# Strassen block products in the up projection of the last layer's MLP of a two-layer diffusion trunk

## The chip, the cores and the metric

The kernel runs on one core of a Trainium2 chip. The metric is the device time in microseconds (us), the median of several runs. A core has five engines with a queue of instructions each, worked through in order: TensorE (PE, with its weight loads shown apart as PEld), VectorE (DVE), ScalarE (ACT), GpSimd (POOL) and SyncE (SP), which here only issues transfers. They wait for each other through semaphores. Sixteen DMA engines carry the transfers.

## The reference

Two layers work on 640 tokens (128 of a prompt, 512 of a sample) of 1024 features. What matters here is step 4 of each layer, a gated MLP with a depthwise convolution over neighbouring tokens; `D_FF` is 2816, and `w_up` has 5632 columns.

```
h2 = _rmsnorm(x, p['norm2']) * (1 + sc2) + sh2
a, g = jnp.split(_dwconv3(h2 @ p['w_up'], p['conv_w'], p['conv_b']), 2, axis=-1)
x = x + g2 * ((jax.nn.silu(a) * g) @ p['w_down'])
```

The convolution is done for the prompt and the sample apart, so nothing crosses the border between token 127 and token 128.

## The kernel before

Activations lie transposed, features on the 128 partitions and tokens along the free dimension. The hidden features come in 22 tile pairs: pair f is a tile of 128 columns of `a` and the tile of `g` that goes with it. Every product is made in three passes (`mm3`): a float32 operand is split into a high part and the small rest, and low times high, high times low and high times high are added up in PSUM.

A weight tile goes through a fixed chain (`load_w`). SP issues one transfer into a staging buffer `st`, ACT copies it to `wh` (the high part), DVE subtracts to get `wl` (the rest), and the matmuls read `wh` and `wl`. There are 3 buffers of `st` and 5 each of `wh` and `wl`, used in turn for all weights of the phase, so at most eight tiles are ahead of PE. A staging buffer is free again when its `wl` is made; a pair of `wh` and `wl` when its last matmul has run.

`mlp_up` does a pair: two weight tiles of 128 by 1024, each with 48 matmuls of 320 columns (2 token halves, 8 blocks of 128 features, 3 passes). ACT takes the sum out of PSUM twice, as `u` and as `v` times the middle tap; DVE adds the outer taps in four instructions (the segments 0 to 127 and 128 to 639 apart); then follow SiLU, the product with the gate, and a split into `ah` and `al`. The down projection (`dn`, and `dl` for the last group) follows each group of 6, 6, 5 and 5 pairs, eight output tiles each, with weights through the same chain. The order on each engine is set by a scheduler that moves instructions ahead as buffers allow.

Beside this, `mod_steps` computes the modulation vectors on DVE from `stm` loads: two DVE instructions of 1024 columns for each of 8 tiles of a group of features. Group 5 (the gate `g2` of the MLP) of the last layer is computed in the last layer's own MLP.

Of the kernel before, what the change touches and what calls it, by code (L numbers as in the profile page):

```python
# [20 lines left out]
P = 128  # L21
# [6 lines left out]
F_T = 22  # L28
EPS = 1e-6
GROUPS = [(0, 6), (6, 12), (12, 17), (17, 22)]  # L30
WINDOWS = (2, 4, 8, 16)
FILL = [[], [('u', 3), ('u', 2), ('u', 1)], [('u', 0), ('g', 16)], [('g', 17), ('g', 18), ('p', 3), ('p', 2)], [('g', 19), ('p', 1), ('p', 0)], [('g', 20), ('g', 8)], [('g', 9), ('g', 10)]]
REST = [('g', 11)]
# [23 lines left out]
def trunk_kernel(ctx: ExitStack, tc: tile.TileContext, a: dict):  # L57
# [10 lines left out]
    wp = tp("wp", 5)  # L68
    dram = (ctx.enter_context(tc.tile_pool(name="dram", bufs=1, space=DRAM)))
    ps_t = tp("ps_t", 2, space=PSUM)  # L70
    ps_a = tp("ps_a", 1, space=PSUM)
    ps_b = tp("ps_b", 1, space=PSUM)

    ident = const.tile([P, P], F32, name="ident")
    make_identity(nc, ident)
# [32 lines left out]
    def load_unit(l, u, eng=vec):  # L108
        return [load_w(a["w_unit"][l, u, c], 768, eng) for c in range(4)]

    def mm3(out, sh, sl, mh, ml, start, stop):
        pe.matmul(out, sl, mh, start=start, stop=False)  # L112
        pe.matmul(out, sh, ml, start=False, stop=False)  # L113
        pe.matmul(out, sh, mh, start=False, stop=stop)  # L114

    def powr(out, x):
        n = x.shape[1]
# [698 lines left out]
    def out_phase(l, x, rp, m32, hp, ps_d):  # L816
# [28 lines left out]
            modulate(rp, x, bc, A2, B2, a0, b0, h2h[c], h2l[c])  # L845
        return h2h, h2l

    def mlp_up(l, f, h2h, h2l, mp, ps_d):
# [21 lines left out]
        va, vg = vs  # L870
        after[0] = vg[:, 0:1]
        act.activation(va, va, AF.Silu)
        vec.tensor_tensor(out=va, in0=va, in1=vg, op=ALU.mult)
        ah = mp.tile([P, T], F32R, tag="ah", name="ah", bufs=8)
        al = mp.tile([P, T], F32R, tag="al", name="al", bufs=8)
        split(va, ah, al)
        return ah, al
# [8 lines left out]
    xst = ExitStack()  # L886
    xp = tp("xp", 1, xst)
    rp = tp("rp", 2, xst)
    x = xp.tile([P, ND, T], F32, name="x")
    hst = ExitStack()  # L890
    hp = tp("h1p", 1, hst, side="right")
# [79 lines left out]
    sst.close()  # L971
    for l in range(L):
        dst.close()
        xst.close()
        attention_phase(l, hh, hl, w0)
        w0 = None
        xst = ExitStack()
        xp = tp("xp", 1, xst)
        rp = tp("rp", 2, xst)
        modp = tp("modp", 1, xst)  # L980
        x = xp.tile([P, ND, T], F32, name="x")
        dst = ExitStack()
        ps_d = open_dense(dst)
        with ExitStack() as ms:
            mp = tp("mg", 1, ms)
            cs = modp.tile([P, 2, 1024], F32, tag="cs", name="cs", bufs=1)
            msteps = mod_steps(l, range(2, 6), modp, cs)
            m32 = merge_phase(l, x, cs, hh, hl, mp, ps_d, msteps)
            hst.close()
            hst = ExitStack()  # L990
            hp = tp("h2p", 1, hst, side="right")
            h2h, h2l = out_phase(l, x, rp, m32, hp, ps_d)
        with ExitStack() as ms:
            mp = tp("mlp", 1, ms)
            ups = {}
            if l + 1 < L:
                msteps = chain(msteps, mod_steps(l + 1, range(2), modp, cs))

            def up_to(f):
                for i in range(len(ups), f):  # L1000
# [4 lines left out]
            for gi, (f0, f1) in enumerate(GROUPS):  # L1005
# [17 lines left out]
                if l + 1 < L:  # L1023
                    hst = ExitStack()
                    hp = tp("h1p", 1, hst, side="right")
                    hh = hp.tile([P, ND, T], F32R, name="hh")
                    hl = hp.tile([P, ND, T], F32R, name="hl")
                    A1 = scale_cols(l + 1, V_N1, 8, "A1")
                for c, (a0, b0) in enumerate(CH_A):
                    acc = Acc(rp, b0 - a0)  # L1030
                    for n0 in range(0, 8, 2):
                        ps = ps_d.tile("dl")
                        for j in range(2):
                            n = n0 + j
                            hi, lo = load_w(a["w_down"][l, n, :, f0 * P:f1 * P], nf * P)
                            for i in range(nf):
                                ks = slice(i * P, (i + 1) * P)
                                mm3(ps[:, j, :b0 - a0], hi[:, ks], lo[:, ks], fs[i][0][:, a0:b0],
                                    fs[i][1][:, a0:b0], i == 0, i == nf - 1)
                            down_add(l, x, n, ps[:, j], a0, b0)  # L1040
                            if l + 1 < L:
                                acc.add(x[:, n, a0:b0], n == 7)
                                dma(x_dram[:, n, a0:b0], x[:, n, a0:b0])
                            else:
                                dma(a["y"][:, n, a0:b0], x[:, n, a0:b0])
                    if l + 1 < L:
                        rms1_chunk(l + 1, c, rp, x, hh, hl, ps_d, acc, A1)
    dst.close()
    xst.close()


# [110 lines left out]
```

## Time and profile before

| what | value |
|---|---|
| device time, three runs | 2299.66 us median (2299.19 to 2304.29) |
| device time of the profiled execution | 2307.55 us |
| span of the profiled execution, first to last instruction | 2305.3 us |
| PE, PEld, DVE, ACT, POOL busy | 97%, 94%, 68%, 42%, 23% of the span |
| last layer's MLP | from 1827 us to the end |

The page of the profile gives busy time by engine, groups of instructions with their mean duration, waits with the engine that ended them, and the transfers with their time from issue to landing. PE records overlap, since matmuls are pipelined: the cost of one matmul in a dense stretch is the stretch divided by its number of matmuls, not the duration of one.

### The profile page before, as it was taken

Reading aid. Unit: us, or ns where it says so; the run is one execution under the profiler, and the core shown is the slowest. Engines: PE = TensorE matmul, PEld = TensorE weight load, DVE = VectorE, ACT = ScalarE, POOL = GpSimd, SP = SyncE. Lnnn points to the kernel's source line nnn. Section 1 sums busy time; section 2 is a strip of 40 time slices with the busy share of each in tenths; the row PEclk is TensorE's granted clock in tenths of the full one; section 3 lists DMA queues with packets and bytes.
Section 4 is the critical chain, followed back from the end, with each engine's and each line's share of the span. In section 5 each row is a group of like instructions: output and inputs, shape, how many; then the busy total and the mean of one; then the engine's idle time right before and its main releaser. Section 6 shows DMA issues by size and latency. Waiting matters only on the chain. (4 is left out here: it accounts for less than half of the span.)

```text
span 2305.3 us, 37922 instructions
## 1 busy us (share of the span) xinstructions
PE 2225.9 (97%) x14778; PEld 2163.6 (94%) x14778; DVE 1562.8 (68%) x2913; ACT 975.7 (42%) x1728; POOL 528.4 (23%) x651
## 2 busy tenths in 40 slices
PE   8898999999999999999979999999999999999999
PEld 4898989989999999999969989899999999999999
DVE  6877687559567756765587867864895676554555
ACT  4555555432244423333355645653323453242422
POOL 3753443024041000000047533320422200000000
PEclk8999999999999999999999999999999999999999
DMA  7211223367333333432242112224762332322123
GB/s 256 80 57 59 82 66 107 108 244 228 121 121 106 101 104 121 135 102 88 75 128 83 57 49 83 97 89 135 283 210 89 123 110 92 94 65 90 50 84 114
DMA packets 102775, 258.50 MB, mean 112 GB/s; under 512 B 19523, under 2 KB 32579, under 8 KB 102596
## 3 DMA queue, kind: packets, MB, share of 16 engines
q1 hardware_dynamic: 102596, 256.09, 34.1%
q8 instruction: 116, 1.90, 0.3%
q14 instruction: 63, 0.51, 0.1%
HBM read 233.10 MB, written 22.95 MB: 111 GB/s over the span
## 5 line engine op out<-in xcount | busy, mean ns | idle before, releaser
L95 ACT ACTIVATE wh<-st 128x1024 fp32r<-128x1024 f32 (+3 forms) x336 | 314.7, 943 | 297.0 <-PE dn L114 170.8
L113 PE MATMUL up<-h2l,wh 128*128 128x320 f32 x1408 | 435.6, 310 | 2.5 <-DVE h2l L209 2.4
L112 PE MATMUL up<-h2h,wl 128*128 128x320 f32 x1408 | 433.5, 310 | 2.4 <-ACT v L862 1.4
L114 PE MATMUL up<-h2h,wh 128*128 128x320 f32 x1408 | 435.0, 310 | 0.0
L96 DVE TENSOR_TENSOR wl<-st,wh 128x1024 fp32r<-128x1024 f32 (+3 forms) x336 | 375.4, 1120 | 71.7 <-ACT wh L95 71.1
L113 PEld LDWEIGHTS up<-h2l,wh 128*128 128x128 f32 x1408 | 265.2, 189 | 3.6 <-DVE h2l L209 3.6
L112 PEld LDWEIGHTS up<-h2h,wl 128*128 128x128 f32 x1408 | 264.5, 189 | 4.0 <-ACT h2h L208 2.1
L114 PEld LDWEIGHTS up<-h2h,wh 128*128 128x128 f32 x1408 | 265.3, 189 | 0.1
L143 DVE SCALAR_TENSOR_TENSOR junk<-stm,cs 128x1024 bf16<-128x1024 f32 x172 | 223.2, 1298 | 60.1 <-DMA stm<-in_w_mod 57.2
L865 DVE SCALAR_TENSOR_TENSOR v<-u,vecs,v 128x127 f32<-128x127 f32 (+1 forms) x176 | 89.1, 547 | 183.4 <-ACT v L862 183.4
L112 PE MATMUL mm<-wh,hl 128*128 128x384 f32 x480 | 169.5, 353 | 15.0 <-ACT raw L361 10.8
L113 PE MATMUL dn<-al,wh 128*128 128x320 f32 x544 | 168.1, 309 | 0.0
L114 PE MATMUL dn<-ah,wh 128*128 128x320 f32 x544 | 168.1, 309 | 0.0
L112 PE MATMUL dn<-ah,wl 128*128 128x320 f32 x544 | 168.1, 309 | 0.0
L113 PE MATMUL mm<-wl,hh 128*128 128x384 f32 x480 | 163.7, 341 | 2.6 <-DVE wl L96 2.6
L114 PE MATMUL mm<-wh,hh 128*128 128x384 f32 x480 | 163.4, 340 | 0.0
L114 PE MATMUL gp<-hh,wh 128*128 128x320 f32 x480 | 148.6, 310 | 0.0
L112 PE MATMUL gp<-hh,wl 128*128 128x320 f32 x480 | 148.4, 310 | 0.0
L113 PE MATMUL gp<-hl,wh 128*128 128x320 f32 x480 | 148.3, 309 | 0.0
L112 PE MATMUL mmu<-hh,wl 128*128 128x384 f32 (+1 forms) x416 | 134.0, 322 | 4.0 <-ACT up L677 2.0
L114 PE MATMUL mmu<-hh,wh 128*128 128x384 f32 (+1 forms) x416 | 131.0, 315 | 0.0
L113 PE MATMUL mmu<-hl,wh 128*128 128x384 f32 (+1 forms) x416 | 130.4, 314 | 0.0
(226 smaller groups left out, 5444.6 us busy)
## 6 DMA issues: line engine op xcount, KB each, us to landing
stm<-in_w_mod SPq DMA_DIRECT2D x88, 512.0 KB, 4.3
st<-in_w_up SPq DMA_DIRECT2D x88, 512.0 KB, 3.6
st<-in_w_gate SPq DMA_DIRECT2D x48, 512.0 KB, 4.4
st<-in_w_unit SPq DMA_DIRECT2D x48, 384.0 KB, 3.2
st<-in_w_out SPq DMA_DIRECT2D x32, 512.0 KB, 3.6
st<-in_w_down SPq DMA_DIRECT2D x48, 320.0 KB, 3.0
st<-in_w_br SPq DMA_DIRECT2D x24, 512.0 KB, 3.6
st<-in_w_down SPq DMA_DIRECT2D x32, 384.0 KB, 3.2
```

What stands on the lines that cost most here:

```text
L95: act.activation(hi, x, AF.Copy)
L96: eng.tensor_tensor(out=lo, in0=x, in1=hi.bitcast(F32), op=ALU.subtract)
L112: pe.matmul(out, sl, mh, start=start, stop=False)
L113: pe.matmul(out, sh, ml, start=False, stop=False)
L114: pe.matmul(out, sh, mh, start=False, stop=stop)
L143: vec.scalar_tensor_tensor(out=junk, in0=st, scalar=1.0, in1=cs[:, j], op0=ALU.mult, op1=ALU.mult, accum_out=col)
L865: vec.scalar_tensor_tensor(out=v[:, s + 1:e], in0=u[:, s:e - 1], scalar=cw[0], in1=v[:, s + 1:e], op0=ALU.mult, op1=ALU.add)
```

## The change

Only the last layer's MLP and its surroundings change. The first 3 of the 22 pairs are computed as before (`plain`). For the other 19, the up projection is seen as a 2 by 2 block product: two rows of weight blocks (the `a` tile and the `g` tile), two halves of the 1024 input features, two halves of the tokens. Eight block products of 12 matmuls become seven, by Strassen's scheme (in Winograd's form). Four products need sums of weight blocks, four need sums of token blocks, and the outputs are sums of the products.

The weight sums are made by transfers. SP loads the first block (128 by 512, 256 KB) into a half of a staging buffer, and POOL then issues accumulating transfers (`accum_op=ALU.add`) that add further blocks to it: one for `s1` and for `s3`, two for `s2`, three for `s4`, each after the one before it. The token sums are made once on DVE and ACT (`tokens`), before the first such pair, with the fourth written over a part of `h2`. The pairs overlap: a step does three products of a new pair and four of the pair before (`step`), on two sets of three PSUM banks. The outputs are put together by DVE and ACT from PSUM; the convolution takes two full-length DVE instructions for a tile in place of four, with small ACT instructions that take away what crossed the border.

Around it, group 5 of the last layer's modulation moves into the first layer's MLP, so 8 steps of `mod_steps` change layers, and some pools are closed earlier.

```diff
+PLAIN = 3
...
+        BUFS = 7
+        SUMS = {"a11": ((0, 0),), "a12": ((0, 1),), "a22": ((1, 1),), "s1": ((1, 0), (1, 1)), "s3": ((1, 0), (0, 0)),
+                "s2": ((1, 0), (0, 0), (1, 1)), "s4": ((0, 1), (1, 0), (0, 0), (1, 1))}
...
+        def tokens(self, tpool):
...
+            for k in range(0, 4, 2):
+                f = {}
+                for i in range(2):
+                    for c in range(2):
+                        f[i, c] = self.mp.tile([P, 2, 320], F32, tag=("ah", "al")[c], name=f"f{i}{c}", bufs=self.BUFS)
+                        ks = slice(4 * i + k, 4 * i + k + 2)
+                        vec.tensor_tensor(out=f[i, c], in0=h[c][:, ks].bitcast(F32), in1=lw[c][:, ks].bitcast(F32),
+                                          op=ALU.add)
+                vec.tensor_tensor(out=f[0, 0], in0=f[0, 0], in1=f[0, 1], op=ALU.subtract)
+                vec.tensor_tensor(out=f[0, 1], in0=f[0, 1], in1=f[1, 1], op=ALU.subtract)
+                vec.tensor_tensor(out=f[1, 1], in0=f[1, 1], in1=f[0, 0], op=ALU.add)
+                vec.tensor_tensor(out=f[1, 0], in0=f[1, 0], in1=f[1, 1], op=ALU.subtract)
+                for q, key in (("n1", (0, 0)), ("t2", (1, 1)), ("n3", (0, 1)), ("n4", (1, 0))):
+                    split(f[key], self.t[q][0][:, k:k + 2], self.t[q][1][:, k:k + 2])
...
+        def weights(self, blocks):
+
+            w = {}
+            for i in range(0, len(blocks), 2):
+                two = blocks[i:i + 2]
+                st = wp.tile([P, 1024], F32, tag="st", name="st", bufs=3)
...
+                for m in range(1, 4):
+                    for at, up in parts:
+                        if m < len(up):
+                            pool.dma_start(at, up[m], accum_op=ALU.add)
+                n = 512 * len(two)
+                split(st[:, :n], hi[:, :n], lo[:, :n])
+                yield w
...
+        def step(self, new):
+
+            h, lw, old = self.h2h, self.h2l, self.pend
+            blocks = []
+            for q, r in (("a11", "a12"), ("s1", "s3"), ("s2", "s4"), (None, "a22")):
+                if new is not None and q:
+                    blocks.append((q, new))
+                if old:
+                    blocks.append((r, old["f"]))
...
+                    elif i == 1:
+                        self.prod(p["d"], block("s1", new), self.t["n1"], True)
+                        vec.tensor_tensor(out=ug[:, 320:], in0=p["d"][:, :320], in1=ug[:, :320], op=ALU.add)
+                    else:
+                        self.prod(p["b"], block("s2", new), self.t["t2"], True)
+                        vec.tensor_tensor(out=ua[:, 320:], in0=p["b"][:, :320], in1=ug[:, :320], op=ALU.subtract)
...
-            msteps = mod_steps(l, range(2, 6), modp, cs)
+            msteps = mod_steps(l, range(2, 6 if l + 1 < L else 5), modp, cs)
...
-            if l + 1 < L:
-                msteps = chain(msteps, mod_steps(l + 1, range(2), modp, cs))
+            msteps = chain(msteps, mod_steps(l + 1, (0, 1, 5), modp, cs))
```

POOL's queue at the end of the program, before: all that follows the norm of the last MLP are eight one-column copies that pace the loads of modulation weights.

```order
L118 TENSOR_TENSOR rr_20026<-ms_20025,mhalf_82 128x2 [waits DVE_49]
L193 TENSOR_TENSOR rr_20026<-ms_20025,mhalf_82 64x1 [waits DVE_49]
L125 COPY stm_20209<-v_20195 128x1 [waits DMAHW5_49,DVE_49,Activation_49]
L125 COPY stm_20348<-v_20335 128x1 [waits DMAHW0_49,DVE_49,Activation_49]
L125 COPY stm_20487<-v_20474 128x1 [waits DMAHW1_49,DVE_49,Activation_49]
```

POOL's queue now, in the third step: the two accumulations of the tile of `s1` and `s3` (`st_20847`), then the five of the tile of `s2` and `s4` (`st_20882`). DMAHW names a semaphore of SP's transfers, DMASW one of POOL's own.

```order
L986 DMA st_20847<-in_w_up 128x512 [waits DMASW7_49,DMAHW4_49,DMASW1_49,DVE_49]
L986 DMA st_20847<-in_w_up 128x512 [waits DMAHW5_49,DMASW3_49]
L986 DMA st_20882<-in_w_up 128x512 [waits DMAHW3_49,DMAHW1_49,DMAHW6_49,DMASW4_49,DVE_49]
L986 DMA st_20882<-in_w_up 128x512 [waits DMAHW7_49]
L986 DMA st_20882<-in_w_up 128x512 [waits DMASW4_49]
L986 DMA st_20882<-in_w_up 128x512 [waits DMASW5_49]
L986 DMA st_20882<-in_w_up 128x512 [waits DMASW7_49]
```

What was a queue of copies is now a queue of 133 accumulations (19 pairs, seven each), in which a later one of a block waits for the earlier one to have landed.

DVE's queue now, where the plain pairs end: the last weight split ahead of the token sums (`wl_20780`, the half tile of the second step), the sums (`f00` to `f11`), and the first low parts (`n11` belongs to the product with `s1`). Before, no such rows stand anywhere.

```order
L98 TENSOR_TENSOR wl_20780<-st_20778,wh_20779 128x512 [waits DMAHW1_49,PE_49,Activation_49]
L960 TENSOR_TENSOR f00_20561<-h2h0_19713,h2l0_19714 128x640
L960 TENSOR_TENSOR f10_20565<-h2h0_19713,h2l0_19714 128x640
L960 TENSOR_TENSOR f00_20581<-h2h0_19713,h2l0_19714 128x640
L960 TENSOR_TENSOR f10_20585<-h2h0_19713,h2l0_19714 128x640
L98 TENSOR_TENSOR al_20552<-v_20478,ah_20551 128x640 [waits Activation_49]
...
L963 TENSOR_TENSOR f01_20583<-f01_20583,f11_20587 128x640 [waits DVE_49]
L98 TENSOR_TENSOR n11_20556<-f00_20561,n10_20555 128x640 [waits Activation_49]
L964 TENSOR_TENSOR f11_20567<-f11_20567,f00_20561 128x640 [waits DVE_49]
L98 TENSOR_TENSOR n11_20556<-f00_20581,n10_20555 128x640 [waits Activation_49]
```

PE's queue now at the same place: after the last plain matmul stand 36 matmuls with `oa` (three products that need no token sums; the last of them are shown), and then the products with `n10` and `n11`.

```order
L117 MATMUL oa_20601<-h2h0_19713,wh_20667 128x320
L115 MATMUL od_20602<-n10_20555,wl_20608 128x320 [waits Activation_49]
L115 MATMUL od_20662<-n10_20555,wl_20701 128x320 [waits DVE_49]
L116 MATMUL od_20602<-n11_20556,wh_20607 128x320 [waits DVE_49]
L117 MATMUL od_20602<-n10_20555,wh_20607 128x320
```

The whole program has 14365 matmul instructions now and 14593 before, 228 fewer.

## Rows read from the trace of the kernel before

**Rows 1.** The page's first part: busy time, share and instructions of each engine.

```profile
PE 2225.9 (97%) x14778; PEld 2163.6 (94%) x14778; DVE 1562.8 (68%) x2913; ACT 975.7 (42%) x1728; POOL 528.4 (23%) x651
```

**Rows 2.** Stretches: the last MLP; a dense stretch of the first; two with many transfers.

```profile
core 0: us, PE busy (x) PEld busy (x) DVE busy (x) ACT busy (x) POOL busy (x), PEclk, DMA share, GB/s
1827.00:2305.00 478.00, 470.81 (x3184) 467.94 (x3182) 268.98 (x469) 173.32 (x229) 10.44 (x12) 1.00 0.28 87
860.00:945.00 85.00, 85.00 (x582) 85.00 (x581) 60.27 (x100) 33.65 (x44) 7.30 (x10) 1.00 0.37 126
0.00:60.00 60.00, 48.90 (x176) 27.17 (x177) 39.38 (x90) 28.25 (x46) 20.46 (x25) 0.83 0.71 253
1600.00:1660.00 60.00, 57.06 (x383) 55.76 (x382) 42.16 (x54) 18.28 (x22) 17.49 (x21) 1.00 0.73 255
```

**Rows 3.** Waits from 1833 us on: SP's own queue, then the engines' longest.

```profile
SPq L102 <- DVE wl L96: 332.5, 62, 27.2
...
DVE v L865 <- ACT v L862: 110.2, 34, 6.2
ACT wh L95 <- PE dn L114: 88.1, 24, 4.5
```

**Rows 4.** DVE and ACT instructions by shape in the last MLP; POOL's copies over the program.

```profile
L96 DVE TENSOR_TENSOR wl<-st,wh 128x1024 fp32r<-128x1024 f32 x39 | 47.6, 1220 | 0.0
L873 DVE TENSOR_TENSOR v<-v 128x640 f32<-128x640 f32 x22 | 18.1, 824 | 0.7
L96 DVE TENSOR_TENSOR al<-v,ah 128x640 fp32r<-128x640 f32 x22 | 18.1, 823 | 12.3 <-ACT ah L95 12.2
L881 DVE SCALAR_TENSOR_TENSOR x<-dn,mod,x 128x320 f32<-128x320 f32 x24 | 13.0, 541 | 0.0
L95 ACT ACTIVATE wh<-st 128x1024 fp32r<-128x1024 f32 x39 | 41.2, 1060 | 59.6 <-PE dn L114 59.6
L125 POOL COPY stm<-v 128x1 f32<-128x1 f32 x32 | 27.3, 869 | 407.9 <-DVE v L867 340.0 <-issue 54.2 <-ACT wh L95 13.7
```

**Rows 5.** Transfers: tile, count, KB of one, median us from issue to landing.

```profile
stm<-in_w_mod SPq DMA_DIRECT2D x88, 512.0 KB, 4.3
st<-in_w_up SPq DMA_DIRECT2D x88, 512.0 KB, 3.6
st<-in_w_down SPq DMA_DIRECT2D x48, 320.0 KB, 3.0
st<-in_w_down SPq DMA_DIRECT2D x32, 384.0 KB, 3.2
x<-x_dram SPq DMA_DIRECT2D x8, 320.0 KB, 5.4
ck<-in_cache_diff_k SPq DMA_DIRECT2D x16, 64.0 KB, 2.3
```

**Rows 6.** SP's issues one behind the other at the start of the program.

```profile
2.50 0.36 SPq L901 DMA_DIRECT2D cs<-in_cond  x1
2.90 0.43 SPq L911 DMA_DIRECT2D cvec<-in_condc  x1
3.37 0.43 SPq L952 DMA_DIRECT2D stk<-in_w_sc  x1
3.84 0.43 SPq L126 DMA_DIRECT2D stm<-in_w_mod  x1
```

More of the change, by code (lines that the diff above doesn't have):

```diff
@@ L70, in trunk_kernel @@
     ps_t = tp("ps_t", 2, space=PSUM)
-    ps_a = tp("ps_a", 1, space=PSUM)
-    ps_b = tp("ps_b", 1, space=PSUM)
+    ab = ExitStack()
+    ps_a = tp("ps_a", 1, ab, space=PSUM)
+    ps_b = tp("ps_b", 1, ab, space=PSUM)
     ident = const.tile([P, P], F32, name="ident")
@@ L109, in load_unit, with mm3 @@
         return [load_w(a["w_unit"][l, u, c], 768, eng) for c in range(4)]
[L111 to L114, printed above, removed]
+    def mm3(out, sh, sl, mh, ml, start, stop, parts=False):
+        pe.matmul(out, sl, mh, start=start, stop=False, skip_group_check=parts)
+        pe.matmul(out, sh, ml, start=False, stop=False, skip_group_check=parts)
+        pe.matmul(out, sh, mh, start=False, stop=stop, skip_group_check=parts)
     def powr(out, x):
@@ L846, in out_phase, with gated @@
         return h2h, h2l
+    def gated(va, vg, mp, bufs):
+        act.activation(va, va, AF.Silu)
+        vec.tensor_tensor(out=va, in0=va, in1=vg, op=ALU.mult)
+        ah = mp.tile([P, T], F32R, tag="ah", name="ah", bufs=bufs)
+        al = mp.tile([P, T], F32R, tag="al", name="al", bufs=bufs)
+        split(va, ah, al)
+        return ah, al
     def mlp_up(l, f, h2h, h2l, mp, ps_d):
@@ L883, in down_add, with mlp_last, down, load @@
                                      op0=ALU.mult, op1=ALU.add)
-    xst = ExitStack()
+    def mlp_last(l, x, h2h, h2l, mp, tpool, ps):
+        m = SevenUp(l, h2h, h2l, mp, ps)
+        ups, n_up = m.ups, 0
+        for gi, (f0, f1) in enumerate(GROUPS):
+            want = min(F_T, f1 + 1)
+            while len(ups) < want:
+                if n_up < PLAIN:
+                    m.plain(n_up)
+                    if n_up == PLAIN - 1:
+                        m.tokens(tpool)
+                else:
+                    m.step(n_up if n_up < F_T else None)
+                n_up += 1
+            fs = [ups[f] for f in range(f0, f1)]
+            nf = f1 - f0
+            last = gi == len(GROUPS) - 1
+            def down(n, w, c0, c1):
+                hi, lo = w
+                o = m.free_bank()
+                for i in range(nf):
+                    ks = slice(i * P, (i + 1) * P)
+                    mm3(o[:, :c1 - c0], hi[:, ks], lo[:, ks], fs[i][0][:, c0:c1], fs[i][1][:, c0:c1],
+                        i == 0, i == nf - 1)
+                return o
+            def load(n):
+                return load_w(a["w_down"][l, n, :, f0 * P:f1 * P], nf * P)
+            if not last:
+                for n in range(8):
+                    w = load(n)
+                    os = [down(n, w, *ch) for ch in CH_B]
+                    for ch, o in zip(CH_B, os):
+                        down_add(l, x, n, o, *ch)
+                continue
+            for c0, c1 in CH_A:
+                for n in range(8):
+                    down_add(l, x, n, down(n, load(n), c0, c1), c0, c1)
+                    dma(a["y"][:, n, c0:c1], x[:, n, c0:c1])
+    xst, rst = ExitStack(), ExitStack()
     xp = tp("xp", 1, xst)
-    rp = tp("rp", 2, xst)
+    rp = tp("rp", 2, rst)
     x = xp.tile([P, ND, T], F32, name="x")
@@ L973, in trunk_kernel @@
         dst.close()
+        rst.close()
         xst.close()
@@ L976, in trunk_kernel @@
         w0 = None
-        xst = ExitStack()
+        xst, rst = ExitStack(), ExitStack()
         xp = tp("xp", 1, xst)
-        rp = tp("rp", 2, xst)
-        modp = tp("modp", 1, xst)
+        rp = tp("rp", 2, rst)
+        modp = tp("modp", 1, rst)
         x = xp.tile([P, ND, T], F32, name="x")
@@ L992, in trunk_kernel @@
             h2h, h2l = out_phase(l, x, rp, m32, hp, ps_d)
+        if l + 1 == L:
+            rst.close()
+            dst.close()
+            ab.close()
+            with ExitStack() as ms:
+                mp = tp("mlp", 1, ms)
+                mlp_last(l, x, h2h, h2l, mp, tp("tsum", 1, ms), tp("ps_o", 1, ms, space=PSUM))
+            break
         with ExitStack() as ms:
@@ L1022, in trunk_kernel @@
                 hst.close()
[L1023 to L1028, printed above, removed]
+                hst = ExitStack()
+                hp = tp("h1p", 1, hst, side="right")
+                hh = hp.tile([P, ND, T], F32R, name="hh")
+                hl = hp.tile([P, ND, T], F32R, name="hl")
+                A1 = scale_cols(l + 1, V_N1, 8, "A1")
                 for c, (a0, b0) in enumerate(CH_A):
@@ L1040, in trunk_kernel @@
                             down_add(l, x, n, ps[:, j], a0, b0)
[L1041 to L1048, printed above, removed]
+                            acc.add(x[:, n, a0:b0], n == 7)
+                            dma(x_dram[:, n, a0:b0], x[:, n, a0:b0])
+                    rms1_chunk(l + 1, c, rp, x, hh, hl, ps_d, acc, A1)
+    hst.close()
     xst.close()
```

108 lines of the change are left out of this document (100 added, 8 removed).

## The prediction

> **What bounds the kernel now.** I first read the page's busy times: PE is busy 97% of the span, DVE 68% [rows 1]. Then the stretches. In the last MLP PE is busy 471 of 478 us, at the full clock; in a dense stretch of the first MLP it is busy for all of 85.00 us, with 582 matmuls [rows 2]. So one matmul of 320 columns costs 85.00 / 582 = 0.146 us, and PE alone sets the pace. The waits show how far the weights are ahead. SP waits 332 us for DVE to free a staging buffer and ACT 88 us for PE to free a pair of `wh` and `wl` [rows 3]: these are waits of a chain that is early, and the eight buffers are full. The last MLP moves only 87 GB/s, at 0.28 of the DMA engines [rows 2]. So removed matmuls are worth their full 0.146 us, as long as the new weight chain keeps up. That is what decides.
>
> **What it removes.** Three plain pairs have 96 matmuls each, 19 others 7 x 12 = 84: 1884 in place of 2112. 228 x 0.146 = **33.3 us less**. A step (84 matmuls) takes 12.3 us of PE.
>
> **The moved modulation steps.** 16 DVE instructions of 1024 columns, about 1.2 us each, go from the last MLP to the first, where DVE is busy 60 of 85 us and PE has no gap [rows 2]. Per pair of 14.0 us there is room for 2.4 us more. Cost 0; if the cover were gone, 16 x 1.2 = 19 us.
>
> **The weight chain, steady part.** The tiles of a step are, in order: T1 (`a11`, `a12`), T2 (`s1`, `s3`), T3 (`s2`, `s4`) and T4, a half tile (`a22`). T1 and T4 need loads only, T2 one accumulation, and T3 three in a row, since each addition to `s4` waits for the one before. With three staging buffers, the T3 of the next step can start only when this step's T3 and T4 are both split: it is the fourth tile on, and three fit. So T3 to T3 is a loop that nothing shortens:
> - Two loads of 256 KB from a freed buffer: SP's second issue begins 0.47 us after the first [rows 6]; landing goes from 3.2 us at 384 KB to 3.0 at 320 KB [rows 5], so an estimated 2.8 at 256 KB. Together 3.3 us.
> - POOL's row: ahead of the first addition to `s4` stand those to the next T2 and to `s2`. POOL's issue of a transfer isn't in the trace. Bounds: SP's 0.47 us [rows 6] and 0.87 us, POOL's one-column copy [rows 4]. The loads of T2 are about 0.7 us ahead of T3's, so this adds 0.5 to 1.8 us.
> - Three accumulations, each A from issue to landing.
> - The split of T3: 1.06 us on ACT and 1.22 on DVE [rows 4], half as much on DVE for T4 (0.6), and 0.5 us for semaphores between them (an allowance of mine). Together 3.4 us.
>
> The loop takes C = 3A + 7.2 to 3A + 8.5 us.
>
> **A.** The trace has no accumulating transfer and none issued by POOL. Below it is bounded by a plain load: 2.3 us for 64 KB, and an estimated 2.8 us for the same 256 KB; above by loads in busier stretches, 4.3 us for 512 KB of modulation weights and 5.4 for `x` [rows 5]. An addition has to read the block and what is already there, twice 256 KB, so I take the `w_up` load that reads 512 KB: **A = 3.6 us** [rows 5]. Then C is 18.0 to 19.3, say 18.7: each step that has to wait for the chain waits 18.7 - 12.3 = 6.4 us.
>
> The Trainium skill speaks for the longer value: in "Collectives: The Full Stack" (The bandwidth ceiling) an add in the DMA engines halves the rate, because it reads two sources; no run here shows it yet. The Trainium skill also has a rule that would give the shorter one: by "DMA: Bandwidth & Descriptors" (Anatomy of one DMA) a transfer issued from GpSimd takes 2.0 us and its bytes at 436 GB/s, an estimated 2.6 us here; the sum would then be between 2287 and 2300 us.
>
> **How many steps wait.** The steps stand in groups of 5, 6, 5 and 4 (the last one computes old products only), with a down projection between. During it the eight buffers fill with the tiles of the next two steps. So n - 2 steps of a group wait. Groups two to four: 4 + 3 + 2 = 9. The first wait of a group is shorter, since `s2` is needed only behind 48 matmuls (7.0 us) and T4 is not waited for (-1.2): 5.8 less. 9 x 6.4 - 3 x 5.8 = **+40 us**.
>
> **The token sums.** After the last plain matmul PE has 36 matmuls (5.3 us) without them. DVE can't begin earlier: ahead of the sums stands a weight split that waits for the `wh` and `wl` of those 36 matmuls. Then come that split (0.6 us, ACT's part about as much) and 14 instructions of 640 columns up to the first `n11`, at 0.82 us [rows 4], 11.5 us. PE stands from 5.3 to 18.1: **+13 us**. The cover is the weight chain: group one's own chains go on in this time, so of its three late steps only the last is late, by about **+3 us**.
>
> **DVE and ACT.** A step costs DVE 3 x 1.22 + 0.6 for splits, 5 reads of 320 columns from PSUM at 0.54 us (the nearest row, `x<-dn`), and 6 instructions of 640 columns at 0.82: 11.9 of 12.3 us [rows 4]. Before, a pair cost it about 8.5 of 14.0. Nearly full, and in order: the split of T3 stands in its queue ahead of the reads of `ob` that free a bank for the next `s3`. When T3 is late, the eviction is too, and the 5.8 us of slack shrink. Between 0 and 3 x 5.8 = 17 us; I take **+5**. The longer conv instructions and the tiny ACT ones lie beside PE (ACT is busy 173 of 478 us [rows 2]). The one accumulation that POOL has ahead of the last norm's `rr` waits for a load that is issued some microseconds earlier; 0.
>
> **Clock.** PE waits of 6 to 13 us may lower the clock: in the first 60 us PE is idle for 11 and the mean clock is 0.83 [rows 2]. A step that waits for its chain has 6 us to take that up. After the token sums it may cost 0 to 2 us; left to the range.
>
> **Sum.** -33.3 + 40 + 13 + 3 + 5 = +28 us. The profiled execution took 2307.55 us, 2.25 more than its span and 0.34% above the median; the difference is carried to the median: 2299.66 + 28 = **2328 us**.
>
> **Rivals.**
> - *The accumulation is a plain transfer.* With A = 2.8 and POOL at 0.47, C = 15.6: 9 x 3.3 - 17 = 12, with the token sums 25, and the total is 2292. With 2.3, C = 14.1, the 9 steps lose 16 and get 17 back: only the token sums stay, 2279. The point from which it decides: A below 2.8. For it: loads here land in 2.3 to 3.6 us with engines that are 0.28 busy [rows 2, 5]. Against it: twice the reads, and four times the transfers of before.
> - *DVE is the bound, not the chain.* At 11.9 of 12.3 us, a tenth more of waiting makes 13.1: 18 steps x 0.8 = 14, with the token sums +27 - 33 = 2293 to 2300, no change. For it: the sum above; against it: DVE's durations are steady over shapes [rows 4].
> - *The DMA engines are full.* A step brings 1.8 MB by loads and adds 1.8 MB. At 253 GB/s with 0.71 busy [rows 2] all engines carry 356 GB/s. If an addition counts twice, 5.5 MB take 15.5 us: 18 x 3.2 = 58 less what is brought ahead in three down stretches (about 8 us each), +34 + 13 - 33 = 2314. If it counts once, 10.3 us, and nothing waits.
> - *The chain is longer still.* A = 4.3 with 0.87 for POOL: C = 21.4, 9 x 9.1 - 17 = 65, group one 13 + 6, DVE 5: 2356. A = 5.4: C = 24.7, 2391.
> - That the change doesn't do what it says: the order of instructions shows the 228 fewer matmuls; only the time of the additions is open.
>
> **How the numbers follow.** The forecast with its longer variant, 2307 to 2391 us: 0.58. Full engines, 2314: 0.08. A plain transfer, 2279 to 2292: 0.22. DVE or a short chain near the break-even: 0.12. A difference of 0.3% (7 us) is about what a measurement of this kernel can tell from none. So faster 0.22, same 0.12, slower 0.66. Most of the cases lie between 2282 and 2385 us; the cases of slower alone between 2307 and 2391.
>
> **What the profile after would show.** The MLP's matmuls 228 fewer, at 0.146 us where dense. A PE gap of about 13 us between the last plain product and the first with `n1`, ended by DVE. In steps three and on of each group, PE waiting some 6 us for `wl` of `s2` and `s4`; DVE and ACT waiting for a transfer on `st`; T3 to T3 18 to 19 us; additions that land 3.6 us after their issue. SP's wait for DVE would no longer be a sign of being early. In down stretches PE without a gap.
>
> Wrong it would be if additions land in 2.5 us (then faster), if POOL takes over 1 us for an issue (slower), or if the scheduler's order on DVE and ACT holds PE up in places that I didn't count.

## Result and profile after

The changed kernel takes 2473.2 us (median of 4; 2468.7 to 2476.7), the kernel before 2301.4 beside it: ratio 1.0745, 95% interval 1.0719 to 1.077. It is slower, as forecast, but by 172 us and not by 28: 145 us above the forecast and outside its range. The last MLP went from 478 to 648 us; it begins some 8 us earlier than before, and the rest of the program kept its time.

The page after, first part (as [rows 1]):

```profile
span 2468.6 us, 38189 instructions
PE 2233.9 (90%) x14550; PEld 2167.6 (88%) x14550; DVE 1644.7 (67%) x2983; ACT 1029.4 (42%) x1868; POOL 647.7 (26%) x784
```

The last MLP as one stretch (as [rows 2], with the columns named there):

```profile
1820.00:2468.00 648.00, 482.82 (x2951) 472.70 (x2951) 332.91 (x505) 227.16 (x369) 117.76 (x136) 0.87 0.61 134
```

The 228 matmuls are gone. PE now stands still for 165 of 648 us, at a mean granted clock of 0.87 where it was 1.00. Longest waits there (engine, line, tile, releaser; us, times, longest; as [rows 3]):

```profile
POOL st L986 <- DMA st<-in_w_up: 337.6, 75, 32.5
DVE wl L98 <- ACT wh L97: 222.1, 64, 12.1
ACT wh L97 <- DMA st<-in_w_up: 211.2, 31, 14.9
...
PE ob L115 <- DVE wl L98: 82.4, 10, 11.0
...
PE od L115 <- DVE ua L1044: 21.8, 4, 9.6
PE od L115 <- DVE wl L98: 18.7, 7, 7.3
PE od L115 <- ACT n L97: 9.9, 1, 9.9
```

Read from the bottom: PE waits for `wl`, DVE's half of a split; DVE waits for ACT's half, ACT for a transfer into `st`; and POOL, which issues the additions, waits for the addition before. Transfers, issue to landing (as [rows 5]): loads by SP, additions by POOL.

```profile
st<-in_w_up SPq DMA_DIRECT2D x133, 256.0 KB, 3.8
st<-in_w_up POOLq DMA_DIRECT2D x133, 256.0 KB, 5.6
```

One step on DVE (groups of splits that hold the tile of `s2` and `s4`, the forecast's T3) and on POOL (the additions of the step that ends at 2119; in brackets the idle time ahead and what ended it):

```profile
2063.09 2.96 DVE L98 TENSOR_TENSOR wl<-st,wh 128x1024 fp32r<-128x1024 f32 x3 [7.26 <-ACT wh L97]
2089.67 2.96 DVE L98 TENSOR_TENSOR wl<-st,wh 128x1024 fp32r<-128x1024 f32 x3 [7.72 <-ACT wh L97]
2118.96 2.96 DVE L98 TENSOR_TENSOR wl<-st,wh 128x1024 fp32r<-128x1024 f32 x3 [7.49 <-ACT wh L97]
2146.22 2.69 DVE L98 TENSOR_TENSOR wl<-st,wh 128x1024 fp32r<-128x1024 f32 x3 [8.85 <-ACT wh L97]
```

```profile
2096.79 0.86 POOL L986 DMA_DIRECT2D st<-in_w_up  x1 [11.44 <-DMA st<-in_w_up]
2098.04 2.68 POOL L986 DMA_DIRECT2D st<-in_w_up  x3 [0.39 <-issue]
2105.81 0.86 POOL L986 DMA_DIRECT2D st<-in_w_up  x1 [5.09 <-DMA st<-in_w_up]
2107.07 0.86 POOL L986 DMA_DIRECT2D st<-in_w_up  x1 [0.40 <-DMA st<-in_w_up]
2113.88 0.86 POOL L986 DMA_DIRECT2D st<-in_w_up  x1 [5.95 <-DMA st<-in_w_up]
```

T3 to T3 is 26.6, 29.3 and 27.3 us, about 27 where the forecast had 18.7. The loop is the one that it described; its pieces are larger. POOL issues four additions in a row up to 2100.7; the next two can go only at 2105.8 and 2107.1, the last at 2113.9, and ACT begins the split at 2117.9: 4.0 us for the last one, which is alone, some 7 for those that share the engines. The loads are slower too. SP issues all five of this step within 2 us, ahead of its additions, and their median landing is 5.6 us:

```profile
st<-in_w_up SPq DMA_DIRECT2D x5, 256.0 KB, 5.6
```

### The profile page after: what moved, and what is told of

Its sections match the earlier page's. It is cut to its first block, busy times and chain, and to the rows that moved or that the text cites. A ratio compares the mean times of both kernels' runs of the same rounds, so it can differ in the third digit from the quotient of the medians.

```text
span 2468.6 us, 38189 instructions
## 1 busy us (share of the span) xinstructions
PE 2233.9 (90%) x14550; PEld 2167.6 (88%) x14550; DVE 1644.7 (67%) x2983; ACT 1029.4 (42%) x1868; POOL 647.7 (26%) x784
## 3 DMA queue, kind: packets, MB, share of 16 engines
q0 software_dynamic: 19152, 34.87, 9.1%
## 5 line engine op out<-in xcount | busy, mean ns | idle before, releaser
L98 DVE TENSOR_TENSOR wl<-st,wh 128x1024 fp32r<-128x1024 f32 (+3 forms) x374 | 410.0, 1103 | 288.8 <-ACT wh L97 288.2
L986 POOL DMA_DIRECT2D st<-in_w_up x133 | 116.1, 941 | 478.6 <-DMA st<-in_w_up 337.6
L116 PE MATMUL up<-h2l,wh 128*128 128x320 f32 x704 | 218.2, 311 | 1.3 <-DVE h2l L212 1.2
L115 PE MATMUL up<-h2h,wl 128*128 128x320 f32 x704 | 217.1, 311 | 1.2 <-ACT v L874 0.7
L117 PE MATMUL up<-h2h,wh 128*128 128x320 f32 x704 | 217.8, 310 | 0.0
L116 PEld LDWEIGHTS up<-h2l,wh 128*128 128x128 f32 x704 | 132.8, 189 | 1.8 <-DVE h2l L212 1.8
L115 PEld LDWEIGHTS up<-h2h,wl 128*128 128x128 f32 x704 | 132.3, 189 | 2.0 <-ACT h2h L211 1.1
L117 PEld LDWEIGHTS up<-h2h,wh 128*128 128x128 f32 x704 | 132.7, 189 | 0.1
L115 PE MATMUL bp<-oh,wl 128*128 128x320 f32 x384 | 117.6, 311 | 3.6 <-DVE m L812 1.8
L116 PE MATMUL bp<-ol,wh 128*128 128x320 f32 x384 | 118.7, 310 | 2.1 <-DVE ol L98 2.1
```

The source lines that it names most:

```text
L115: pe.matmul(out, sl, mh, start=start, stop=False, skip_group_check=parts)
L116: pe.matmul(out, sh, ml, start=False, stop=False, skip_group_check=parts)
L117: pe.matmul(out, sh, mh, start=False, stop=stop, skip_group_check=parts)
L986: pool.dma_start(at, up[m], accum_op=ALU.add)
```

## The experiments

The theory: the additions, and the loop of load, three additions and split through three staging buffers, cost all that is lost. The rivals: the new frame of the MLP, DVE, the row of transfers on POOL whatever they do, and full DMA engines. Each ratio below is to the kernel before, run beside it.

### What the parts cost

**Frame alone.** All 22 pairs are computed as before, in the new frame.

```diff
-PLAIN = 3
+PLAIN = 22
-                    if n_up == PLAIN - 1:
-                        m.tokens(tpool)
```

> All 22 pairs are plain in the new frame (its tiles, banks, conv of 640 columns, moved modulation steps), with no sums at all. Theory (the frame costs nothing, the loss is all in the seven products): 2295 to 2310 us. Rival (the frame itself, with three banks a turn and the longer DVE instructions, costs some of it): 2320 to 2350 us.

2300.7 us, ratio 0.9989 (0.9979 to 0.9999). Frame, banks, longer DVE instructions and the moved modulation steps cost nothing.

**No additions.**

```diff
-                            pool.dma_start(at, up[m], accum_op=ALU.add)
+                            pass
```

> The accumulating transfers are left out, so each weight sum is only its first block (the output is not the reference's); loads, splits, matmuls, token sums and their order stay. Theory (the chain through the additions costs nearly all): the pair-to-pair loop shrinks below 12.3 us of PE, the long waits of PE on wl vanish, and the time is 2307 - 33 + 11 (token sums) + 0 to 10 = 2275 to 2300 us; additions then cost 175 to 200 us. Rival (DVE and ACT with their new order are the bound, additions matter little): 2380 us or more.

2282.7 us, ratio 0.991 (0.9894 to 0.9926). The additions cost 190 us, and DVE as the bound is out: its work is unchanged in this run.

**Token sums early** (made after plain pair 0; only the split of `n4` stays behind the last), with the additions and without.

```diff
+                    if n_up == 0:
+                        m.tokens(tpool, 0)
                     if n_up == PLAIN - 1:
-                        m.tokens(tpool)
+                        m.tokens(tpool, 1)
```

> The token sums are made after the first plain pair and not after the third; only the last split (n4, which writes over the plain operands) stays behind the third. Theory (PE's stand behind the last plain matmul, 11.2 us in the changed kernel, is the wait for the 28 or so DVE instructions of the sums): that gap goes, 2458 to 2466 us. Rival (the weight chain of the first step ends at about the same time, so another wait takes the place): 2470 to 2476 us.

> The additions left out (2282.7 us by itself; the sums are not made, the output is not the reference's) and the token sums early. Theory (without a chain the gap of 11 us behind the last plain matmul is all on the path): 2270 to 2274 us, which is all that the removed matmuls can bring, 2303 - 33. Rival (the sums cost the same elsewhere): 2280 to 2284 us.

With additions 2472.2 us, against 2473.2: no gain, as the rival said, though the gap of 11.2 us at the first `n11` is gone from PE's row. Without them 2274.9 (ratio 0.9896, 0.9873 to 0.9919), 7.8 less than late and just above the theory's range. So the gap is on the path only where no chain is later still.

**Plain transfers in place of additions.**

```diff
-                            pool.dma_start(at, up[m], accum_op=ALU.add)
+                            pool.dma_start(at, up[m])
```

> Each accumulating transfer becomes a plain transfer from POOL of the same block to the same place (the sums are not made; the output is not the reference's); the number of transfers, their issue on POOL and the wait of each for the one before stay. Theory (an addition is slow because it has to read what is there: a low rate, and it slows the loads beside it): a plain transfer lands in 2.5 to 3.5 us, and most of the loss goes: 2300 to 2350 us. Rival (what costs is the row of transfers on POOL and the wait of one for the next, whatever they do): at least 2420 us.

2358.3 us, ratio 1.0243 (1.0224 to 1.0262), a little over the theory's range. Of the 190 us, 76 are the row of transfers and its loop, and 115 come from the fact that the transfers add. The run also answers what a landing time of 3.5 us gives, which is nearly the forecast's A of 3.6. Its page has POOL's issues (count, busy us, mean ns, idle before) and the transfers:

```profile
L986 POOL DMA_DIRECT2D st<-in_w_up x133 | 71.7, 540 | 408.5 <-DMA st<-in_w_up 305.4
...
st<-in_w_up SPq DMA_DIRECT2D x133, 256.0 KB, 3.6
st<-in_w_up POOLq DMA_DIRECT2D x133, 256.0 KB, 3.5
```

ACT's splits that hold T3, in group two of this kernel:

```profile
2046.40 2.52 ACT L97 ACTIVATE wh<-st 128x1024 fp32r<-128x1024 f32 x3 [3.91 <-DMA st<-in_w_up]
2067.22 2.52 ACT L97 ACTIVATE wh<-st 128x1024 fp32r<-128x1024 f32 x3 [4.04 <-DMA st<-in_w_up]
2088.04 2.31 ACT L97 ACTIVATE wh<-st 128x1024 fp32r<-128x1024 f32 x3 [4.24 <-DMA st<-in_w_up]
```

20.8 us a step. With 3 x 3.5 that leaves 10.3 us for the rest of the loop; in the changed kernel 27 - 3 x 5.6 = 10.2. So C = 3A + 10 fits both, where the forecast had 3A + 7.2 to 8.5.

### What makes an addition slow

**Half of each sum, and a shorter row.** The second gives `s1`, `s3` and `s2` two additions each and `s4` one.

```diff
-                            pool.dma_start(at, up[m], accum_op=ALU.add)
+                            pool.dma_start(at[:, :256], up[m][:, :256], accum_op=ALU.add)
```

```diff
-        "s1": ((1, 0), (1, 1)), "s3": ((1, 0), (0, 0)),
-        "s2": ((1, 0), (0, 0), (1, 1)), "s4": ((0, 1), (1, 0), (0, 0), (1, 1))}
+        "s1": ((1, 0), (1, 1), (0, 0)), "s3": ((1, 0), (0, 0), (1, 1)),
+        "s2": ((1, 0), (0, 0), (1, 1)), "s4": ((0, 1), (1, 0))}
```

> Each addition takes only the first 256 of a block's 512 columns: the same number of transfers and the same row, half the bytes (half of each sum is left out; the output is not the reference's). Theory (a low rate of the adding transfers, and their crowding): A falls from 5.6 to about 4 us and the time to 2380 to 2410 us. Rival (fixed costs of each addition, its issue on POOL and its latency): 2450 us or more; with fixed costs alone POOL's issue stays at 0.86 to 0.94 us.

> Seven additions a step as before, but two each for s1, s3 and s2 and one for s4, so that no sum has three in a row (the values of s1, s3 and s4 are other sums; the output is not the reference's). Theory (the row of additions sets the loop): one addition of 5.6 us less a step in 13 to 15 steps that wait, 2380 to 2410 us. Rival (the bytes that are added set it, whatever their row): 2455 us or more.

Half the bytes: 2382.0 us (ratio 1.0335, 1.0316 to 1.0353), landing 3.7 us, POOL's issue still 0.86. The same bytes with rows of two: 2409.1 us (1.045, 1.0433 to 1.0466), landing 5.9. Both runs lie in their theories' ranges: the bytes count, and so does the length of the row.

**By size.** The frame with 22 plain pairs, each with a load and three additions in a row into tiles that nobody reads.

```diff
+            for m in range(3):
+                for p in pb:
+                    pool.dma_start(p[:, :n], src[:, :n], accum_op=ALU.add)
```

> The frame with 22 plain pairs (2300.7 us), and in each pair, into tiles that nobody reads, a load and three additions in a row issued by POOL: by turns one row of 256 KB additions, two such rows side by side, one of 512 KB and one of 128 KB. Nothing waits for them, so the time should stay within 1% of 2300 us. Theory: a 256 KB addition by itself takes about 4.0 us and two side by side 5 to 6 each; 512 KB takes 6 to 7, 128 KB about 3. Rival (a fixed cost): all between 3.5 and 4.5 us whatever the size, and no longer side by side.

Transfers in the last MLP, KB and median us to landing:

```profile
pb512x<-in_w_up POOLq DMA_DIRECT2D x54, 256.0 KB, 4.2
pb1024x<-in_w_up POOLq DMA_DIRECT2D x15, 512.0 KB, 5.6
pb256x<-in_w_up POOLq DMA_DIRECT2D x15, 128.0 KB, 3.1
```

So an addition of 256 KB takes 4.2 us where fewer transfers run, and 5.6 in the changed kernel. The row of 256 KB mixes additions that go one at a time (median 4.1 us from 1990 us on) with a part up to 1960 us where two rows often run side by side (median 4.5, under the 5 to 6 expected). My claim that nothing waits was wrong: the run took 2386.4 us (one run), because SP's load into such a tile waits for the additions of the one before (152, 102 and 58 us by size), with the weight loads queued behind it. The run is used for landing times only.

**Engine time.** The DMA queues in the last MLP (packets, MB, share of 16 engines over the stretch), of the changed kernel and of the one with plain transfers:

```profile
q0 software_dynamic: 19152, 34.87, 34.5%
q1 hardware_dynamic: 27189, 51.60, 25.9%
```

```profile
q1 hardware_dynamic: 27355, 52.16, 30.7%
q0 software_dynamic: 10640, 34.87, 20.5%
```

q0 is POOL's. 133 additions take 0.345 x 648 / 133 = 1.68 us of all engines each; the plain transfers 0.205 x 536 / 133 = 0.83. An addition counts twice. The Trainium skill says as much of the add in a ReduceScatter, by its two source reads, in "Collectives: The Full Stack" (The bandwidth ceiling), and the runs agree. With 7 loads at 0.85 (0.259 x 648 us for 51.6 MB) a step needs 7 x 1.68 + 7 x 0.85 = 17.7 us of full engines, already more than PE's 12.3.

### How many steps wait

**Five staging buffers, and four pairs of split buffers**; then the early token sums as well.

```diff
-    wp = tp("wp", 5)
+    wp = tp("wp", 4)
-                st = wp.tile([P, 1024], F32, tag="st", name="st", bufs=3)
+                st = wp.tile([P, 1024], F32, tag="st", name="st", bufs=5)
```

> Five staging buffers in place of three, and four pairs of split buffers in place of five (the same room). Everything is computed. With five buffers the next step's additions can begin while this step's tiles still wait for their splits. Theory (the loop through three staging buffers, load, three additions, split, sets 27 us a step): chains of two steps overlap, and the time falls to 2370 to 2430 us. Rival (the additions that overlap slow each other, so more of them under way brings nothing): 2445 us or more.

> Five staging buffers (2361.9 us by themselves) and the early token sums (2472.2 by themselves, no gain) together. Theory (the gap behind the last plain matmul was hidden because the chain of the first step was later still): with the faster chain the gap is partly on the path, 2352 to 2358 us. Rival (it is never on the path): 2360 to 2364 us.

2361.9 us (ratio 1.0253, 1.0233 to 1.0274), 111 less and below the theory's range, and that although PE begins the last MLP late, at 1831.3 us (1819.3 in the changed kernel). The loop through three buffers was the longer bound; the next one is the engines. Two steps of this kernel, and three in a row with them:

```profile
2040.00:2057.00 17.00, 13.13 (x84) 12.35 (x84) 10.50 (x16) 8.11 (x15) 6.01 (x7) 1.00 0.99 217
2057.00:2074.00 17.00, 13.13 (x84) 12.34 (x84) 10.93 (x16) 8.53 (x15) 5.40 (x7) 1.00 0.94 207
2040.00:2091.00 51.00, 38.93 (x244) 36.83 (x245) 31.00 (x45) 23.81 (x41) 13.13 (x15) 0.98 0.84 186
```

A step takes 17 us, against the 17.7 worked out, with the DMA engines 0.99 and 0.94 busy; in the third POOL issues only two additions, which lowers the share of the three to 0.84. The early sums bring nothing here either (2365.3 us, ratio 1.0278, 1.0261 to 1.0296), against my expectation: at the first late sum of group one PE stands 6.7 us earlier than with late sums (1928.8 and 1935.4 us), at the third step of group two only 1.0 (2034.2 and 2035.2). That fits steps in between that go at the additions' pace.

**Down weights out of the way.** Is anything brought ahead in a down projection? POOL's waits in the first one of the changed kernel:

```profile
POOL st L986 <- DVE wl L98: 30.6, 1, 30.6
POOL st L986 <- DMA st<-in_w_up: 9.3, 4, 4.7
```

For 30.6 us no addition is issued, to the split of a late down tile: the eight down tiles go through the same `st`, `wh` and `wl`, and their splits wait for PE. So the first three projections were made with one tile of weights:

```diff
-                for n in range(8):
-                    w = load(n)
+                w = load(0)
+                for n in range(8):
```

> The changed kernel, but in the first three down projections all eight blocks use the weights of the first (seven of eight loads and splits left out; the output is not the reference's). Theory (the forecast's two steps brought ahead in each down stretch of 35 to 42 us do not come about because the down weights hold the staging and split buffers till PE has used them): now the additions run through the stretch, about 25 us less in each of three, 2385 to 2410 us. Rival (the staging loop is as slow during the stretch, or the buffers hold no more than one step): 2445 us or more.

2444.8 us (ratio 1.0624, 1.0606 to 1.0642): 28 less, 9.5 a stretch. It is at the edge of the rival: the down tiles are a cause, and a smaller one than I thought. In group two PE's waits of over 4 us go from five (4.9 to 11.0 us) to four, the forecast's n - 2. By the traces the steps of groups two to four are 44 us shorter together, while the down stretches are 16 longer, with waits of PE for DVE's `x`. POOL's standing by itself proves little, since with one down tile it still stands for 23.9 us in the first stretch. What differs is PE: the first two sums `s2` of group two are used 12.3 us apart, PE's own pace, and 21.3 us apart in the changed kernel.

### Covering the loop, or taking it elsewhere

**Every other pair plain** (ten pairs as seven products, 26.3 us of PE for each chain; `n4` in tiles of its own; four staging and four split buffers).

```diff
-PLAIN = 3
+SEVEN = range(2, 21, 2)
...
+                if n_up in SEVEN or n_up >= F_T:
+                    m.step(n_up if n_up < F_T else None)
+                else:
+                    m.plain(n_up)
```

> Only ten pairs (2, 4, ... 20) are made as seven products, and a plain pair stands between any two of them; the token sums are made after the first pair and have a place of their own, four staging buffers and four pairs of split buffers. Everything is computed. Theory (one chain needs 20 to 27 us and PE can give it 12.3 + 14.0 = 26.3 us, so nothing waits): the saved matmuls come back, 10 x 12 x 0.146 = 17.5 us less than before, 2284 to 2293 us. Rival (the additions also hold up the loads of the plain pairs and of the down projection, which share the staging buffers): 2303 us or more.

2355.5 us (ratio 1.0236, 1.0219 to 1.0252), in the rival's range. PE no longer waits long for a sum, yet it waits. ACT's row at the end of one such wait:

```profile
2029.31 0.42 ACT L927 ACTIVATE u<-ob 128x320 f32<-128x320 f32 x1
2036.97 1.06 ACT L97 ACTIVATE wh<-st 128x1024 fp32r<-128x1024 f32 x1 [7.25 <-DMA st<-in_w_up]
2037.93 0.91 ACT L936 ACTIVATE v<-u,vecs 128x640 f32<-128x640 f32 x1
2038.74 0.42 ACT L927 ACTIVATE u<-oa 128x320 f32<-128x320 f32 x1
```

And PE's, in the same place:

```profile
2039.21 0.64 PE L115 MATMUL oa<-h2h,wl 128*128 128x320 f32 x1 [5.08 <-ACT u L927]
```

The split of a late sum stands in ACT's queue ahead of the eviction of `oa`, which PE needs to go on. So the late split went to POOL, once with these buffers, and once with the old ones (three staging, five split, two of `v`):

```diff
+                if any(len(up) > 2 for _, up in parts):
+                    pool.tensor_copy(hi[:, :n], st[:, :n])
+                    pool.tensor_tensor(out=lo[:, :n], in0=st[:, :n], in1=hi[:, :n].bitcast(F32), op=ALU.subtract)
```

> The ten alternating pairs (2355.5 us) with the split of the late tile (s2 and s4) made by POOL in place of ACT and DVE. Everything is computed. Theory (ACT and DVE take their instructions in order, and the split of the late sum holds up evictions behind it, gaps of 4 to 6 us a pair): these gaps go, 2300 to 2320 us; what then remains over 2284 is the room taken from the split buffers, 7 to 12 us ahead of the MLP. Rival (the gaps are the transfers' own lateness): 2345 us or more.

> The same with the staging and split buffers of the kernel before (three and five) and two buffers of v in place of three. Theory: without the loss ahead of the MLP 2288 to 2305 us. Rival (with three staging buffers the loop of load, three additions of 4.2 us, POOL's split and the plain pair's two tiles is over the 26.3 us that PE has): 2320 us or more.

2328.7 us (ratio 1.012, 1.0097 to 1.0142) and 2334.3 us (1.0145, 1.013 to 1.016). 27 us come back with the first, so the queue order is a real cause. Its time lies between theory and rival; the second is in its rival's range, and neither beats the kernel before.

**Sums made in DRAM during the first layer's MLP.** Four sums a pair by four copies and four additions, 512 KB each for two pairs, with `s2` from `s1` and `s4` from `s2`; the last MLP only loads.

```diff
+                dma(s1, blk(f, 1, 1))
+                dma(s3, blk(f, 0, 0))
...
+                pool.dma_start(s1, blk(f, 1, 0), accum_op=ALU.add, max_dma_last_dim=8192)
+                pool.dma_start(s3, blk(f, 1, 0), accum_op=ALU.add, max_dma_last_dim=8192)
...
+                pool.dma_start(s2, s1, accum_op=ALU.add, max_dma_last_dim=8192)
...
+                pool.dma_start(s4, s2, accum_op=ALU.add, max_dma_last_dim=8192)
```

> All of it is computed: 19 pairs as seven products, token sums early, and the four sums of a pair made in DRAM beforehand, two pairs to a transfer of 512 KB, in the first layer's MLP (s2 from s1, s4 from s2: four additions and four copies a pair in place of seven additions). Theory (only the place of the additions was wrong): the last MLP is as fast as with the additions left out (2274.9 us) and the first MLP, whose DMA engines are 0.3 busy, takes them without a wait: 2272 to 2285 us. Rival (the copies and additions, some 40 MB more for the DMA engines, delay the first MLP's own loads): 2295 us or more.

2398.2 us (ratio 1.0415, 1.0396 to 1.0434), for a reason that I had not named. The page's slices (tenths busy, 60 us each):

```profile
PE   4319999999999999999998999999999999999999
...
DMA  9995112223753333333425211222485323343434
```

Nothing held these transfers back, so they ran at the start (POOL issues the first at 1.3 us), beside the first loads, and PE lost the time there. Now each block waits for one element of the first MLP's `v`, and all are issued by POOL:

```diff
+                for s in (s1, s3, s2, s4):
+                    pool.dma_start(s[0, 0:1, 0:1], after[0][0:1])
```

> As the run before (all computed, sums made in DRAM), but the first transfer into each block of sums is one element of the first MLP's `v`, so that the copies and additions that follow it are spread over the pairs of that MLP, all issued by POOL. Theory (place, not cost): nothing waits at the start nor in the first MLP, 2272 to 2290 us, faster than before. Rival (DMA engines too busy in the first MLP, or POOL's queue holds up the modulation copies): 2303 us or more.

2289.3 us (ratio 0.995, 0.9937 to 0.9964): in the theory's range, 0.5% faster than the kernel before, clear of the noise, and 184 us faster than the change. The copies and additions that read `w_up`:

```profile
s<-in_w_up POOLq DMA_DIRECT2D x54, 512.0 KB, 10.2
```

The first MLP as a stretch, and below it the same of the kernel with early sums and no additions:

```profile
692.00:1178.00 486.00, 472.31 (x3189) 469.20 (x3188) 331.12 (x581) 181.59 (x250) 108.63 (x168) 0.99 0.71 197
692.00:1169.00 477.00, 472.04 (x3195) 469.17 (x3193) 329.61 (x582) 181.03 (x251) 39.91 (x48) 1.00 0.36 117
```

These transfers land in 10.2 us, and it hardly matters. The first MLP pays with one gap of 9.5 us on PE: a down projection waits for DVE, which had itself waited 8.0 us for a load of modulation weights. That is nearly all of the 10 us by which the whole span (2283.4) is over that of the kernel with early sums and no additions (2273.3).

## Why the prediction was wrong

**Right: what would bound.** The matmuls went, the frame and the moved steps cost nothing, the loop T3 to T3 was the bound, and PE waited for `wl`. Removed matmuls and token sums together were put at 2299.7 - 33.3 + 13 = 2279.4; without additions 2282.7 was measured. So nearly the whole error, 142 of 145 us, is in the additions: forecast +40, +3 and +5 = 48 us, measured 2473.2 - 2282.7 = 190.

The traces of the changed kernel and of the one without additions show where it lies. A stretch goes from its first matmul to the first of the next one; us:

| stretch of the last MLP | without additions | changed kernel | longer by | forecast |
|---|---|---|---|---|
| plain pairs and steps, group one | 102 | 133 | 31 | 3 |
| steps, group two | 74 | 141 | 67 | 20 |
| steps, group three | 62 | 107 | 45 | 13 |
| steps, group four | 44 | 83 | 39 | 7 |
| the four down stretches | 160 | 169 | 9 | 0 |

The forecast's +5 for DVE and ACT has no place in it, and the last MLP begins 4 us earlier.

**The step that failed: the size of the loop, through A.** A was put at 3.6 us, the row of a 512 KB load [rows 5]. Measured: 4.2 where fewer transfers run, 5.6 in place. The row was chosen for twice the bytes. An addition does cost twice the engine time, but it also shares the engines: up to four are under way at once, and the first of them run beside loads. The rest of the loop was 10 us and not 7.2 to 8.5. Loads land in 3.8 us (2.8 estimated; 3.0 without additions), and in 5.6 where five are issued together, as above; POOL's issue is 0.86 to 0.94, at its upper bound or a little over. So C is 27 in place of 18.7, of which 3 x 2.0 = 6.0 is A. The run with one down tile shows what this is worth, since there the steps wait as the forecast had it, n - 2 in a group: its steps of groups two to four are 107 us longer than without additions, where the forecast had 40. The forecast's own sum with C = 27 gives 9 x 14.7 - 17 = 115. The size of the loop is thus 67 us of the error.

The Trainium skill's formula in "DMA: Bandwidth & Descriptors" (Anatomy of one DMA), an estimated 2.6 us, is further off: the shortest median of an addition of this size in these runs is 4.1, and POOL's plain transfers took 3.5.

**How many steps wait.** The count n - 2 assumed that a down projection leaves the buffers to the next two steps. It does not: the second step of group two already waits, and with one down tile it doesn't. The steps of groups two to four are 151 us longer in the changed kernel and 107 with one down tile, so this is 44 us (28 in the time of that run, whose down stretches are longer).

**Group one** was put at +3, since its chains would run on behind the token sums. It is 31 us longer: PE waits 7.1 us for `ug` at 1880, 7.5 and 8.5 for `wl`, and 1.3 besides, 24 in all; the other 7 are slower matmuls, at a mean granted clock of 0.85 in this stretch and 0.93 without additions. That is 28 us more than forecast.

These three and the down stretches make 67 + 44 + 28 + 9 = 148 us; less the 5 that was put down for DVE and ACT and the 4 of the earlier start it is 139, and the spans of the two kernels differ by 140 more than the forecast's 48. The kernel with plain transfers agrees: with the forecast's A, nearly, it takes 2358 and not 2328.

**DVE and ACT, +5.** As the bound DVE is out. The order in its queue that the forecast feared is in the changed kernel: behind a late split stands `ua`, which reads a bank that PE needs.

```profile
2035.65 1.23 DVE L98 TENSOR_TENSOR wl<-st,wh 128x1024 fp32r<-128x1024 f32 x1 [10.66 <-ACT wh L97]
2036.80 0.48 DVE L1044 TENSOR_TENSOR ua<-od,ua 128x320 f32<-128x320 f32 x1
2037.33 0.64 PE L115 MATMUL od<-n,wl 128*128 128x320 f32 x1 [7.13 <-DVE ua L1044]
```

In the alternating pairs such waits are worth 27 us. In the changed kernel 21.8 us of PE's waits end on `ua`, but their cost was not measured apart: PE would soon have waited for the late sum itself.

**Token sums, +13.** The gap was 11.2 us, but it didn't add: with the chain behind it, taking it away brought nothing.

**Clock, 0.** The granted clock is 0.87 in the last MLP, and PE's busy time is 41 us over that of the kernel without additions (2192.8) for the same 14550 matmuls. Most of it lies in steps whose length the chain sets, which agrees with "absorbed". Not all of it does: group one's 7 us are named above, and the second down stretch, right behind the longest waits, takes 48.0 us for what a dense one does in 42.2, with 3.3 us of waiting.

```profile
2155.50:2203.50 48.00, 44.70 (x290) 44.47 (x290) 22.22 (x39) 10.57 (x16) 7.87 (x9) 0.94 0.57 136
```

No run takes the clock out alone.

**The rivals.** The plain transfer (A below 2.8) did not come. Full engines were named at 15.5 us a step; measured were 17.7 of demand and 17 in the run with five buffers, so that rival is the next bound behind the loop. The longer chain had the right form (A = 5.4, C = 24.7) but ended at 2391, for want of 2.3 us a step, of the waits behind the down stretches and of those in group one.

## What to carry to other kernels

When a transfer gets a new kind of work and stands in a loop, measure it crowded, as it will run, before counting on any row of a lone, plain transfer; and multiply an error in it by its place in the loop (here three). A loop through few buffers is priced by everything that passes through them, the tiles of the next stage too. And ask first whether the work must be on the path: the same sums, made by four additions a pair and paced into a stretch whose DMA engines were 0.36 busy, turned 172 us of loss into 13 of gain, some 8 of them from the early token sums (7.8 without additions).

## What the runs showed of the hardware

An accumulating transfer of 256 KB takes 1.68 us of all 16 DMA engines (changed kernel) and a plain one to the same place 0.83. It lands in 4.2 us where fewer transfers run; 128 KB in 3.1, 512 KB in 5.6 (the run by size). POOL's issue is 0.54 us for a plain transfer (10640 / 133 = 80 packets) and 0.86 to 0.94 for an addition (19152 / 133 = 144 packets), also for one of half the bytes, whose packets are as many. In the run by size the 84 additions have 12096 packets, 144 each, and an issue takes 0.87 to 0.88 us for 128, 256 and 512 KB when nothing is issued right behind it: in these runs issue time went with packets, not bytes.
